# Three resumes fewer before the first convolution taps, block 0's transposes in the auxiliary banks, and a pair as first unit of the first paired feed-forward block

## The chip, the cores and the metric

The kernel runs on one core of a Trainium2 chip. The metric is the device time of one execution in microseconds. Before the change three runs gave a median of 1071.13 us (1070.79 to 1071.79). TensorE is called PE below, VectorE DVE, ScalarE ACT, GpSimd POOL, and the queue that issues nearly all DMAs SP.

## The reference

One layer of a hybrid encoder for a sequence of 256 rows of 2048 numbers, all in float32:

```python
xn = rms_norm(h, norm1_g[l])
proj = xn @ w_in                       # 5120 columns: q, k, v, ga, gg
att = diff_attention(rope(norm(q)), rope(norm(k)), v, lam)
u = ga * sigmoid(gg)                   # 1024 channels
u = causal_depthwise_conv(u, conv_w[l], conv_b[l])   # 31 taps
u = silu(layer_norm(u, conv_ln_g[l], conv_ln_b[l]))
h = h + concat([att, u]) @ w_out
hn = rms_norm(h, norm2_g[l])
h = h + (silu(hn @ w_gate) * (hn @ w_up)) @ w_down   # FFN_HIDDEN = 5632
```

## The kernel before, in words

**The matrix products.** The 256 rows are two row tiles m of 128. A weight is read from HBM once, in chunks of two k-tiles of 128 by 512 columns. Each chunk is split into a rounded part `hi` (ACT, L313) and the rest `lo = raw - hi` (DVE, L322); the activations are split in the same way. A product is then three matmuls, xhi by hi, xlo by hi (L352, L353) and xhi by lo (L358). A chunk has 12 matmuls of 512 columns on PE: eight in its first half, which need `hi` alone, and four in its second, which need `lo`.

**The order.** It is written out by the program itself: each engine runs its own list in the order in which the Python code emits it. `run_chunks` goes through a list of chunks; before the multiplication of chunk t it emits the load, the rounding and the splitting of chunks some places ahead (`lead`: 2 for plain chunks, 3 and 2 for the units of a paired block). What follows a block of products (gates, norms, transposes) stands in Python generators. `resume()` advances each running generator by one `yield`; it is called twice in a chunk, after the first and after the second half, so a `yield` is a delay of half a chunk in PE's list. `lag(n)` is n such delays. A chunk whose `prompt` is set gets one more `resume()` right behind its last one.

**Convolution.** The first four blocks of `w_in` give the gated channels, 256 at a time. `glu_done` takes a sigmoid (ACT), a product `u` (DVE, L475), transposes `u` on PE (`ps_u`, L483) and copies it to the padded buffer `upad` (ACT). From there on the 31 taps of each channel tile are queued in `side`, and DVE runs one tap (L495, 30 per channel tile, 240 in all) after the other between its other work, as a budget of DVE time per half chunk allows. When four channel tiles are through, `conv_back` transposes them back (`ps_y`, L516), and after the second four it takes the layer norm: statistics (DVE, L526 and L535), the reciprocal root (POOL, L210 to L540), scale and shift (ACT, L544), transposes (`ps_ln`, L553), SiLU (ACT, L557) and the split into `mchi` and `mclo` (DVE, L560, L561). The last chunks of `w_out` multiply `mchi` and `mclo`. The function `operand` emits what is missing of them right there, in front of the matmul that reads them.

**Feed-forward.** 5632 hidden columns are 11 blocks j of 512, in groups of 4, 4 and 3; after a group its rows of `w_down` are multiplied. Block 0 is plain: 8 chunks of `w_gate`, 8 of `w_up`, then `up_done` forms `a = up * rstd * silu(gate)` (DVE, L796), and `transposed` transposes it (`ps_a`, L809), rounds it (ACT, L811) and subtracts (DVE, L813). All other blocks are made by `fast_block` from 12 units: four `s` units (pairs), which multiply 4 k-tiles by 7 products of sums of operands (one level of a Strassen-like scheme over the two halves of k and the two weights), and four `g` and four `u` units, which are plain chunks of the other k-tiles. A pair has 21 matmuls on PE. It needs a 1 MB load (`wb`, two DMAs, L880), sums of the weights `wt` (DVE, L890 to L892), two roundings `wh` (ACT, L893 of `wb`, L896 of `wt`) and two subtractions `wl` (DVE, L898, L899). The operand side (`fhi`, `flo`, `chi`, `clo`) is made once, by `make_forms`, while block 0 runs. It reads the normed rows `hn`, whose two tiles lie in the two buffers that `wb` uses afterwards.

**PSUM.** Four banks `acc` and four banks `aux`. Plain blocks take two `acc` banks; a paired block takes the four `acc` banks for the products Q1, Q6, Q7, Q5 and the four `aux` banks for Q2, Q4, Q3, QX. Transposes use `aux`, but those of block 0 use `acc`.

```python
FIRST = "gugsgsusgsuu"      # units of block 1
ORDER = "sggsggsuusuu"      # units of blocks 2 to 10
PRODUCTS = ((Q1, 0, 5), (Q6, 5, 1), (Q7, 6, 2), (Q5, 4, 3), (Q2, 1, 6), (Q4, 3, 0), (Q3, 2, 4))
```

In `PRODUCTS` the third number is the row of `wh` and `wl` that is read: rows 4 to 6 come from L893 and L898, rows 0 to 3 from L896 and L899.

Of the kernel before, what the change touches and what calls it, by code (L numbers as in the profile page):

```python
# [12 lines left out]
F32 = mybir.dt.float32  # L13
# [5 lines left out]
P = 128  # L19
D = 2048  # L20
S = 256
# [49 lines left out]
FGROUPS = (4, 4, 3)  # L71
# [7 lines left out]

ORDER = "sggsggsuusuu"  # L80

FIRST = "gugsgsusgsuu"

Q1, Q6, Q7, Q5, Q2, Q4, Q3, QX = range(8)

PRODUCTS = ((Q1, 0, 5), (Q6, 5, 1), (Q7, 6, 2), (Q5, 4, 3), (Q2, 1, 6), (Q4, 3, 0), (Q3, 2, 4))

HI_AHEAD, LO_AHEAD = 3, 2

FIRSTS = [1] + [sum(FGROUPS[: g + 1]) for g in range(len(FGROUPS))]  # L90


def rope_constants():
# [10 lines left out]
def tile_block(  # L104
# [16 lines left out]
    acc_ps = ctx.enter_context(tc.tile_pool(name="acc", bufs=4, space=PSUM))  # L121
    aux_ps = ctx.enter_context(tc.tile_pool(name="aux", bufs=AUX, space=PSUM))
# [28 lines left out]
    def col(key, k):  # L151
        return cols[:, AT[key] + k : AT[key] + k + 1]
# [67 lines left out]
    def lhs_two(pfx, k):  # L220
        return tuple(lhs.tile([P, 2, S], F32R, tag=f"l{x}", name=f"{pfx}{x}{k}") for x in ("hi", "lo"))
# [21 lines left out]
    def lag(n):  # L243
        for _ in range(n):
            yield
# [4 lines left out]
    def room(n, hold=0):  # L250
        while held[0] + n > AUX:
            yield
        held[0] += hold
# [6 lines left out]
    def spend(us):  # L260
        credit[0] -= us
# [16 lines left out]
    chunks = []  # L278
# [182 lines left out]
    def glu_done(c0, nct, ps):  # L461

        w = nct * P
        while not normed:
            yield
        yield
        sig = []
        for m in range(NM):
            sig.append(pre.tile([P, HN], F32, tag="p1", name="sig"))
            act.activation(sig[m][:, :w], ps[m][:, :w], AF.Sigmoid, scale=rstd1[m])  # L470
        yield from lag(2)
        us = []
        for m in range(NM):
            u = pre.tile([P, HN], F32, tag="wt", name="u", bufs=4)
            dve.scalar_tensor_tensor(u[:, :w], ps[m][:, w:], rstd1[m], sig[m][:, :w], ALU.mult, ALU.mult)  # L475
            us.append(u)
        spend(0.25)
        yield from lag(3)
        yield from room(1)
        pt = aux_ps.tile([P, 2, S], F32, tag="aux", name="ps_u")  # L480
        for j in range(nct):
            for m in range(NM):
                pe.transpose(pt[:, j, m * P : (m + 1) * P], us[m][:, j * P : (j + 1) * P], ident)  # L483
        act.copy(upad[c0 // NB][:, c0 % NB : c0 % NB + nct, W - 1 :], pt[:, :nct])
        yield
        cts = range(c0, c0 + nct)
        for ct in cts:
            act.activation(y[:, ct, :], upad[ct // NB][:, ct % NB, :S], AF.Identity,  # L488
                           bias=col("cb", ct), scale=cw[:, ct, :1])
            side.append(deque((lambda k=k, ct=ct: tap(k, ct)) for k in range(1, W)))  # L490
# [298 lines left out]

    def up_done(j, ps):  # L790
        fp = ffn["pool"]
        yield
        aa = []
        for m in range(NM):
            a = fp.tile([P, N], F32, tag=f"sum{2 + m}", name="a")
            dve.scalar_tensor_tensor(a, ps[m], rstd2[m], sil[m], ALU.mult, ALU.mult)  # L796
            aa.append(a)
        yield
        yield from transposed(j, aa)

    def transposed(j, aa):
        last = j + 1 in FIRSTS
        for t in range(N // P // 2):
            pool_, tag = (aux_ps, "aux") if j else (acc_ps, "acc")
            pt = pool_.tile([P, 2, S], F32, tag=tag, name="ps_a")
            for i in range(2):
                for m in range(NM):
                    c = (2 * t + i) * P
                    pe.transpose(pt[:, i, m * P : (m + 1) * P], aa[m][:, c : c + P], ident)  # L809
            hi, lo = lhs_two("a", j * (N // P) + 2 * t)  # L810
            act.copy(hi, pt)  # L811
            yield from lag(1 if last else 2)
            dve.tensor_tensor(lo, pt, hi.bitcast(F32), ALU.subtract)  # L813
            for i in range(2):
                actT[j * (N // P) + 2 * t + i] = (hi[:, i, :], lo[:, i, :])
            yield from lag(1 if last else 4)
# [202 lines left out]
    c0 = 0  # L1019
    for nct in CONV_BLOCKS:  # L1020
        block(w_in, [(GC + c0 * P, nct * P), (AC + c0 * P, nct * P)], range(KD), fx,
              lambda ps, c0=c0, nct=nct: glu_done(c0, nct, ps))
# [13 lines left out]
    j0 = 0  # L1036
    for g, nb in enumerate(FGROUPS):
        for j in range(j0, j0 + nb):
            if j:
                fast_block(j, FIRST if j == 1 else ORDER, j == j0)  # L1040
                continue

            block(w_gate, j * N, range(KD), fh, silu_done)
            block(w_up, j * N, range(KD), fh, lambda ps, j=j: up_done(j, ps))
        for n in range(D // N):
            at = len(chunks)
            block(w_down, n * N, range(j0 * 4, (j0 + nb) * 4), fa, lambda ps, g=g, n=n: down_done(g, n, ps))
            for i, c in enumerate(chunks[at:]):
                c["prompt"] = True
                c["spare_raw"] = i % 3 == 2  # L1050
        j0 += nb
# [32 lines left out]
```

## Time and profile before

| what | value |
|---|---|
| median of 3 runs | 1071.13 us |
| the profiled execution | 1070.95 us, its span 1069.2 us, so 1.75 us lie around the span |
| busy, share of the span | ACT 55%, POOL 6%, DMA packets 62% of 16 engines' span |
| mean granted PE clock | 0.997 |
| convolution taps on DVE | 240 of 480 ns |

In rows of the timeline the first number is the start in us from the span's start, the second the duration, then engine, line, operation, output and inputs with their shapes and the count; in square brackets the idle time of that engine just before, and what ended it. Matmuls are pipelined: one of 512 columns shows about 0.39 us, and the next starts 0.227 us after it. A wait list has the engine and line that waited, what it waited for, and us in total, times, longest. A window table has, for each stretch, its length, the busy time of each engine with the number of instructions, the granted PE clock, the DMA share and GB/s.

### The profile page before, as it was taken

To read this page: it belongs to the slowest core of one execution; us is meant where nothing else is said; L and a number is where in the kernel's file an instruction comes from. 1 tells how busy PE (TensorE), PEld (TensorE's weight loads), DVE (VectorE), ACT (ScalarE), POOL (GpSimd) and SP (SyncE) were. 2 spreads that over 40 slices of the span, in tenths; PEclk is the share of its full clock that TensorE was granted. 3 is DMA by queue.
4 is the path that set the end of the run, shared out by engine and by line. 5 is a ranking of instruction groups with operands and counts; after the bars stand their busy time and mean duration, and the time that the engine had idled before them with its cause. 6 is when DMAs were issued, how large, how long until landed. Compare 5 with 4: busy or idle time off the path is not lost.

```text
span 1069.2 us, 13025 instructions
## 1 busy us (share of the span) xinstructions
PE 1052.4 (98%) x4738; PEld 865.6 (81%) x4738; DVE 842.8 (79%) x1022; ACT 588.8 (55%) x761; POOL 64.5 (6%) x101
## 2 busy tenths in 40 slices
PE   9999999999899998999999999999999999999998
PEld 7888888877688886778888888888888888888886
DVE  5699899898765589999664599999964579998653
ACT  6654566756656555466443465765643356646332
POOL 0030112201100000000000000000000000000000
PEclk9999999999999999999999999999999999999999
DMA  8756655544435556577555667867656568676661
GB/s 280 243 185 199 203 161 177 158 159 157 158 103 190 177 189 223 202 241 203 191 181 205 236 204 250 250 193 247 178 182 210 199 219 273 205 234 188 196 240 60
DMA packets 116812, 212.43 MB, mean 199 GB/s; under 512 B 7188, under 2 KB 25038, under 8 KB 116748
## 3 DMA queue, kind: packets, MB, share of 16 engines
q1 hardware_dynamic: 113616, 200.56, 55.7%
q0 software_dynamic: 3072, 11.01, 5.6%
q8 instruction: 37, 0.61, 0.2%
q14 instruction: 27, 0.22, 0.1%
q10 hardware_dynamic: 60, 0.03, 0.0%
HBM read 200.04 MB, written 2.10 MB: 189 GB/s over the span
## 4 chain that ended last, share of the span: by engine, by line
PE 84%; DVE 8%; ACT 3%; issue 2%; DMA 1%; POOL 1%; SPq 1%; DVEq 0%; ACTq 0%
PE acc L358 16%; PE acc L352 16%; PE acc L353 16%; PE q L932 6%; PE q L933 6%; PE q L938 6%; PE q L917 5%; PE q L915 5%; PE q L916 5%; DVE wlo L322 2%; DVE y L495 1%; PE ps_a L809 1%; ACT wh L896 1%; ACT whi L313 1%; DMA wb<-in_w_gate_dram 1%
## 5 line engine op out<-in xcount | busy, mean ns | idle before, releaser
L322 DVE TENSOR_TENSOR wlo<-raw,whi 128x1024 fp32r<-128x1024 f32 x278 | 337.6, 1222 | 141.7 <-ACT whi L313 141.6
L313 ACT CAST whi<-raw 128x1024 fp32r<-128x1024 f32 x296 | 309.1, 1052 | 235.3 <-PE acc L353 169.8
L352 PE MATMUL acc<-whi,ahi 128*128 128x512 f32 x384 | 150.0, 391 | 0.0
L353 PE MATMUL acc<-whi,alo 128*128 128x512 f32 x384 | 149.5, 389 | 0.0
L352 PE MATMUL acc<-whi,xhi 128*128 128x512 f32 x320 | 126.3, 395 | 0.6 <-ACT whi L313 0.4
L932 PE MATMUL q<-whi,chi 128*128 128x512 f32 x320 | 125.5, 392 | 0.0
L353 PE MATMUL acc<-whi,xlo 128*128 128x512 f32 x320 | 125.0, 391 | 0.3 <-DVE xlo L227 0.3
L933 PE MATMUL q<-whi,clo 128*128 128x512 f32 x320 | 124.7, 390 | 0.0
L896 ACT CAST wh<-wt 128x2048 fp32r<-128x2048 f32 x40 | 76.6, 1915 | 76.8 <-DVE wt L892 76.8
L915 PE MATMUL q<-wh,fhi 128*128 128x512 f32 x280 | 109.8, 392 | 0.7 <-DVE alo L813 0.7
L917 PE MATMUL q<-wl,fhi 128*128 128x512 f32 x280 | 109.2, 390 | 0.8 <-DVE wl L899 0.8
L916 PE MATMUL q<-wh,flo 128*128 128x512 f32 x280 | 109.0, 389 | 0.0
L495 DVE SCALAR_TENSOR_TENSOR y<-upad,cw,y 128x256 f32<-128x256 f32 x240 | 102.2, 480 | 2.6 <-ACT y L488 2.6
L358 PE MATMUL acc<-wlo,ahi 128*128 128x512 f32 x384 | 102.9, 389 | 0.0
L899 DVE TENSOR_TENSOR wl<-wt,wh 128x2048 fp32r<-128x2048 f32 x40 | 91.6, 2290 | 9.1 <-ACT wh L896 9.1
L358 PE MATMUL acc<-wlo,xhi 128*128 128x512 f32 x320 | 87.8, 396 | 0.9 <-DVE wlo L322 0.9
L938 PE MATMUL q<-wlo,chi 128*128 128x512 f32 x320 | 86.7, 393 | 0.0
L353 PEld LDWEIGHTS acc<-whi,alo 128*128 128x128 f32 x384 | 72.1, 188 | 14.9
L352 PEld LDWEIGHTS acc<-whi,ahi 128*128 128x128 f32 x384 | 72.1, 188 | 14.9
L358 PEld LDWEIGHTS acc<-wlo,ahi 128*128 128x128 f32 x384 | 72.0, 188 | 14.9
L352 PEld LDWEIGHTS acc<-whi,xhi 128*128 128x128 f32 x320 | 60.1, 188 | 13.7 <-ACT whi L313 0.8
L353 PEld LDWEIGHTS acc<-whi,xlo 128*128 128x128 f32 x320 | 60.1, 188 | 13.4 <-DVE xlo L227 1.1
(194 smaller groups left out, 1417.1 us busy)
## 6 DMA issues: line engine op xcount, KB each, us to landing
raw<-in_w_down_dram SPq DMA_DIRECT2D x88, 512.0 KB, 3.9
raw<-in_w_in_dram SPq DMA_DIRECT2D x48, 512.0 KB, 3.6
raw<-in_w_gate_dram SPq DMA_DIRECT2D x48, 512.0 KB, 4.6
raw<-in_w_up_dram SPq DMA_DIRECT2D x48, 512.0 KB, 3.6
wb<-in_w_up_dram SPq DMA_DIRECT2D x40, 512.0 KB, 3.8
wb<-in_w_gate_dram SPq DMA_DIRECT2D x40, 512.0 KB, 5.5
raw<-in_w_in_dram SPq DMA_DIRECT2D x64, 256.0 KB, 3.9
raw<-in_w_out_dram SPq DMA_DIRECT2D x32, 512.0 KB, 3.6
```

Source lines behind the costliest of these rows:

```text
L313: act.copy(c["hi"], c["raw"])
L322: dve.tensor_tensor(c["lo"], c["raw"], c["hi"].bitcast(F32), ALU.subtract)
L352: pe.matmul(ps[m], xhi[:, ms], hi[:, j, :], start=c["first"] and j == 0, stop=False)
L353: pe.matmul(ps[m], xlo[:, ms], hi[:, j, :], start=False, stop=False)
L358: pe.matmul(ps[m], xhi[:, ms], lo[:, j, :], start=False, stop=c["last"] and j == nk - 1)
L495: dve.scalar_tensor_tensor(y[:, ct, :], src, wk, y[:, ct, :], ALU.mult, ALU.add)
L915: pe.matmul(ps, fhi[:, f, p, :], c["hi"][:, w], start=bool(first), stop=False)
L916: pe.matmul(ps, flo[:, f, p, :], c["hi"][:, w], start=False, stop=False)
L917: pe.matmul(ps, fhi[:, f, p, :], c["lo"][:, w], start=False, stop=bool(last))
L932: pe.matmul(ps, x1[:, ms], hi[:, i, :], start=i == 0 and bool(c["first"].get(q)), stop=False)
L933: pe.matmul(ps, x2[:, ms], hi[:, i, :], start=False, stop=False)
L938: pe.matmul(sum_bank(c, q), forms["plain"][k][0][:, ms], lo[:, i, :], start=False, stop=i == 1 and bool(c["last"].get(q)))
```

## The change

Four edits:

1. For the first convolution block (c0 = 0) `glu_done` yields once instead of twice before `u` and once instead of three times before the transposes. Those stand 3 half chunks earlier in PE's list, directly behind the second half of the chunk that holds the transposes of the tap weights. All later work of the taps moves with it, as the queue of taps starts earlier.
2. `up_done` of block 0 has lost its `yield` at the start and its chunk is now `prompt`, so `a` is emitted right behind the last chunk; the transposes follow after `lag(4)` instead of one `yield`. They lie in `aux` banks.
3. `FIRSTS` no longer holds 1, so `transposed` of block 0 uses the longer delays (2 and 4) of the other blocks.
4. Block 1 has the unit order of all other blocks and begins with a pair instead of three plain units.

```diff
-FIRST = "gugsgsusgsuu"
-FIRSTS = [1] + [sum(FGROUPS[: g + 1]) for g in range(len(FGROUPS))]
+FIRSTS = [sum(FGROUPS[: g + 1]) for g in range(len(FGROUPS))]
...
             act.activation(sig[m][:, :w], ps[m][:, :w], AF.Sigmoid, scale=rstd1[m])
-        yield from lag(2)
+        yield from lag(2 if c0 else 1)
...
-        yield from lag(3)
+        yield from lag(3 if c0 else 1)
         yield from room(1)
         pt = aux_ps.tile([P, 2, S], F32, tag="aux", name="ps_u")
...
     def up_done(j, ps):
         fp = ffn["pool"]
-        yield
         aa = []
...
-        yield
+        yield from lag(4)
         yield from transposed(j, aa)
...
-            pool_, tag = (aux_ps, "aux") if j else (acc_ps, "acc")
-            pt = pool_.tile([P, 2, S], F32, tag=tag, name="ps_a")
+            pt = aux_ps.tile([P, 2, S], F32, tag="aux", name="ps_a")
...
-                fast_block(j, FIRST if j == 1 else ORDER, j == j0)
+                fast_block(j, ORDER, j == j0)
...
             block(w_up, j * N, range(KD), fh, lambda ps, j=j: up_done(j, ps))
+            chunks[-1]["prompt"] = True
```

How the lists move, at three places. The line numbers of the changed kernel are 2 to 4 lower.

DVE, end of the convolution, from the split of the last attention rows (`alo`) to the first operand of the convolution's product (`mchi`); before:

```order
L227 SCALAR_TENSOR_TENSOR alo_2771<-ps_at,cols,ahi_2770 128x256 x2
L495 SCALAR_TENSOR_TENSOR y<-upad_123,cw,y 128x256 x6
L322 TENSOR_TENSOR wlo<-raw,whi 128x1024
L495 SCALAR_TENSOR_TENSOR y<-upad_123,cw,y 128x256
L322 TENSOR_TENSOR wlo<-raw,whi 128x1024 x3
L526 BN_STATS stats_127<-upad_123 128x6
L526 BN_STATS stats_128<-upad_123 128x6
L322 TENSOR_TENSOR wlo<-raw,whi 128x1024
L535 BN_AGGR mv<-stats_127 128x2
L535 BN_AGGR mv<-stats_128 128x2
L322 TENSOR_TENSOR wlo<-raw,whi 128x1024 x2
L560 CAST mchi_2938<-z 128x256
```

and in the changed kernel:

```order
L225 SCALAR_TENSOR_TENSOR alo_2778<-ps_at,cols,ahi_2777 128x256 x2
L320 TENSOR_TENSOR wlo<-raw,whi 128x1024 x3
L524 BN_STATS stats_127<-upad_123 128x6
L524 BN_STATS stats_128<-upad_123 128x6
L533 BN_AGGR mv<-stats_127 128x2
L533 BN_AGGR mv<-stats_128 128x2
L320 TENSOR_TENSOR wlo<-raw,whi 128x1024 x2
L558 CAST mchi_2914<-z 128x256
```

The last seven taps (`y`) are gone from this place, as they ran earlier, and two chunk splits (`wlo`) fewer lie between `alo` and `mchi`.

PE, the last matmuls with attention rows (`alo`, `ahi`) and the first with the convolution's rows (`mchi`); before:

```order
L353 MATMUL acc<-whi,alo_2771 128x512
L358 MATMUL acc<-wlo,ahi_2770 128x512 x4
L553 MATMUL ps_ln<-ident,upad_122 128x128 x4
L352 MATMUL acc<-whi,mchi_2938 128x512
L353 MATMUL acc<-whi,mclo_2939 128x512
```

and in the changed kernel:

```order
L551 MATMUL ps_ln<-ident,upad_122 128x128 x4
L356 MATMUL acc<-wlo,ahi_2777 128x512 x4
L551 MATMUL ps_ln<-ident,upad_123 128x128 x4
L350 MATMUL acc<-whi,mchi_2914 128x512
L351 MATMUL acc<-whi,mclo_2915 128x512
```

The first fence's `ps_ln` is the first of four; in the second fence stand the second and the third, and the first stands a first half (eight matmuls) ahead of its top row. The transposes `ps_y` ahead of all this stand one and a half chunks earlier, so that five whole chunks lie between them and the first matmul with `mchi`, where there were three and the second half of one.

DVE, from the last of the operand forms (`flo`) to the second pair of block 1; before:

```order
L874 TENSOR_TENSOR flo<-sums,fhi 128x1536
L322 TENSOR_TENSOR wlo<-raw,whi 128x1024 x5
L890 TENSOR_TENSOR wt<-wb 128x1024
L891 TENSOR_TENSOR wt<-wb,wt 128x512
L892 TENSOR_TENSOR wt<-wt,wb 128x512
L322 TENSOR_TENSOR wlo<-raw,whi 128x1024
L796 SCALAR_TENSOR_TENSOR a<-acc,rstd_0_135,sil 128x512
L796 SCALAR_TENSOR_TENSOR a<-acc,rstd_1_136,sil 128x512
L898 TENSOR_TENSOR wl<-wb,wh 128x1536
L899 TENSOR_TENSOR wl<-wt,wh 128x2048
L813 TENSOR_TENSOR alo_3871<-ps_a,ahi_3870 128x512
L322 TENSOR_TENSOR wlo<-raw,whi 128x1024
```

and in the changed kernel:

```order
L870 TENSOR_TENSOR flo<-sums,fhi 128x1536
L320 TENSOR_TENSOR wlo<-raw,whi 128x1024 x3
L886 TENSOR_TENSOR wt<-wb 128x1024
L887 TENSOR_TENSOR wt<-wb,wt 128x512
L888 TENSOR_TENSOR wt<-wt,wb 128x512
L894 TENSOR_TENSOR wl<-wb,wh 128x1536
L895 TENSOR_TENSOR wl<-wt,wh 128x2048
L320 TENSOR_TENSOR wlo<-raw,whi 128x1024
L793 SCALAR_TENSOR_TENSOR a<-acc,rstd_0_135,sil 128x512
L793 SCALAR_TENSOR_TENSOR a<-acc,rstd_1_136,sil 128x512
L886 TENSOR_TENSOR wt<-wb 128x1024
L887 TENSOR_TENSOR wt<-wb,wt 128x512
```

The first pair's work (`wt`, `wl`) now directly follows the splits of the last three chunks of `w_up`, and `a` stands behind it and one more split.

## The prediction, made before the changed kernel had run

> **What bounds the kernel now.** I read the page's busy times first, then PE's list of waits, then the granted clock around the long waits, then the timeline there.
>
> ```profile
> span 1069.2 us, 13025 instructions
> ...
> PE 1052.4 (98%) x4738; PEld 865.6 (81%) x4738; DVE 842.8 (79%) x1022; ACT 588.8 (55%) x761; POOL 64.5 (6%) x101
> ```
>
> PE is busy for all but 16.8 us of the span and the change removes none of its matmuls, so only PE's stops can be won. PE's longest waits:
>
> ```profile
> PE acc L352 <- DVE mchi L560: 3.3, 1, 3.3
> PE ps_a L809 <- DVE a L796: 3.1, 2, 2.8
> ...
> PE q L917 <- DVE wl L899: 0.8, 1, 0.8
> PE q L915 <- DVE alo L813: 0.7, 1, 0.7
> ...
> PE ps_a L809 <- DVE sum L997: 0.3, 1, 0.3
> ```
>
> The first lies at the end of the convolution, the others around block 1; the change touches both places. Busy time hides a second cost, which the window table shows (the column after POOL is the granted clock):
>
> ```profile
> 287.10:290.50 3.40, 1.71 (x9) 1.00 (x7) 0.00 (x0) 3.40 (x5) 0.00 (x0) 1.00 0.47 172
> 290.50:293.90 3.40, 1.56 (x6) 1.11 (x7) 2.48 (x5) 1.24 (x3) 0.00 (x0) 1.00 0.00 1
> 293.90:297.30 3.40, 3.40 (x12) 2.71 (x11) 0.51 (x2) 1.02 (x2) 0.00 (x0) 0.50 0.00 0
> 403.10:406.50 3.40, 0.57 (x4) 0.15 (x2) 3.33 (x6) 2.16 (x3) 0.00 (x0) 1.00 0.78 295
> 406.50:409.90 3.40, 3.11 (x9) 2.40 (x10) 3.40 (x3) 2.83 (x3) 0.00 (x0) 0.51 0.03 8
> ```
>
> After each of the two long waits PE runs for 3.4 us at half its clock, which does 1.7 us less work. The window ahead of the slow one was busy for 1.56 and 0.57 us of 3.4; one with 1.71 us was not followed by a slow one. The two slow windows start 112.6 us apart, 33 times 3.41, so they lie on a fixed grid. I take half a window of idleness as the limit.
>
> **The change part by part.**
>
> *End of the convolution.* PE, then DVE:
>
> ```profile
> 278.00 1.04 PE L516 MATMUL ps_y<-ident,y 128*128 128x128 f32 x8
> ...
> 284.36 1.07 PE L358 MATMUL acc<-wlo,ahi 128*128 128x512 f32 x4
> ...
> 287.08 1.07 PE L358 MATMUL acc<-wlo,ahi 128*128 128x512 f32 x4
> ...
> 288.53 0.55 PE L553 MATMUL ps_ln<-ident,upad 128*128 128x128 f32 x3 [0.27 <-ACT upad L544]
> ...
> 292.34 0.49 PE L352 MATMUL acc<-whi,mchi 128*128 128x512 f32 x1 [3.26 <-DVE mchi L560]
> ```
>
> ```profile
> 269.40 1.27 DVE L495 SCALAR_TENSOR_TENSOR y<-upad,cw,y 128x256 f32<-128x256 f32 x3
> ...
> 273.14 2.46 DVE L495 SCALAR_TENSOR_TENSOR y<-upad,cw,y 128x256 f32<-128x256 f32 x6
> ...
> 276.65 0.48 DVE L495 SCALAR_TENSOR_TENSOR y<-upad,cw,y 128x256 f32<-128x256 f32 x1
> ...
> 292.00 0.28 DVE L560 CAST mchi<-z 128x256 fp32r<-128x256 f32 x1
> ```
>
> From `ps_y` (278.00) to the end of the first `mchi` (292.28) the chain of copy, statistics, root, shift, `ps_ln`, SiLU and cast takes 14.3 us. A chunk is 287.08 - 284.36 = 2.72 us of PE, so a matmul 0.227. In the new list `ps_y` stands 1.5 chunks earlier: 2.72 + 8 x 0.227 = 4.5 us, at 273.5. The taps allow it: the seven taken away here are those from 273.14 to 277.13, the last one left ends at 270.7. PE then has 0.8 (ps_y) + 5 x 2.72 + about 3 x 0.45 (three ps_ln) = 15.75 us of work before it needs `mchi`, 1.4 us more than the chain, in which two splits fewer now stand. So this stop goes. It cost 0.4 us of the interrupted `ps_ln`, then 292.34 less the 288.86 at which three transposes would have been through = 3.5, and 1.7 of clock: **5.6 us won**. Bounds: if the chain grew by 3 us, PE would stop for 1.6 and the clock might stay up, 4.0 won; the whole 5.6 is the most.
>
> *Opening.* The price of the earlier taps. PE, then DVE:
>
> ```profile
> 39.07 1.20 PE L358 MATMUL acc<-wlo,xhi 128*128 128x512 f32 x4
> ...
> 44.67 0.60 PE L483 MATMUL ps_u<-ident,u 128*128 128x128 f32 x4
> ```
>
> ```profile
> 39.28 0.87 DVE L475 SCALAR_TENSOR_TENSOR u<-acc,rstd,sig 128x256 f32<-128x256 f32 x2
> ...
> 47.05 1.67 DVE L495 SCALAR_TENSOR_TENSOR y<-upad,cw,y 128x256 f32<-128x256 f32 x4 [2.60 <-ACT y L488]
> ```
>
> `ps_u` now comes behind that L358, at 39.07 + 4 x 0.227 = 39.98, while the second `u` ends at 40.15: PE waits about 0.2, **0.2 lost** (bounds 0 and 0.5). ACT's copy of `ps_u`, which now waits there, holds up one rounding by less than a chunk, and roundings run two chunks ahead of PE. The first seven taps go into the 2.60 us in which DVE waited; as DVE's list between 47 and 270 is the same mixture, only seven taps ahead, I give it nothing.
>
> *Block 1: what goes.* PE:
>
> ```profile
> 398.89 0.39 PE L932 MATMUL q<-whi,chi 128*128 128x512 f32 x1
> ...
> 403.20 0.39 PE L933 MATMUL q<-whi,clo 128*128 128x512 f32 x1
> 406.41 0.36 PE L809 MATMUL ps_a<-ident,a 128*128 128x128 f32 x1 [2.83 <-DVE a L796]
> 407.07 0.90 PE L809 MATMUL ps_a<-ident,a 128*128 128x128 f32 x3 [0.29 <-DVE a L796]
> ...
> 415.86 0.50 PE L915 MATMUL q<-wh,fhi 128*128 128x512 f32 x1 [0.71 <-DVE alo L813]
> ...
> 460.16 0.50 PE L917 MATMUL q<-wl,fhi 128*128 128x512 f32 x1 [0.84 <-DVE wl L899]
> ```
>
> Idle counts from a modelled end, some 0.15 us after the next matmul could have started. Start to start, with 0.227 for a matmul and 0.1 for a transpose: 3.0 and 0.55 before `ps_a`, 1.7 of clock, 0.85 and 1.0 at the two last rows and 0.4 at the wait for L997: 7.5 us. In the new order `ps_a` stands behind a whole pair, when `a` is long done.
>
> *Block 1: what comes.* The pair now meets PE at 398.9, when `w_up` ends, instead of behind three plain units. DVE, ACT, and the landing times of `wb`:
>
> ```profile
> 384.61 1.28 DVE L869 TENSOR_TENSOR flo<-hn,fhi 128x512 fp32r<-128x512 f32 x2
> ...
> 391.12 4.62 DVE L322 TENSOR_TENSOR wlo<-raw,whi 128x1024 fp32r<-128x1024 f32 x4
> ...
> 401.88 1.23 DVE L890 TENSOR_TENSOR wt<-wb 128x1024 f32<-128x1024 f32 x1 [3.73 <-DMA wb<-in_w_gate_dram]
> ...
> 405.61 1.40 DVE L796 SCALAR_TENSOR_TENSOR a<-acc,rstd,sil 128x512 f32<-128x512 f32 x2
> 406.93 1.75 DVE L898 TENSOR_TENSOR wl<-wb,wh 128x1536 fp32r<-128x1536 f32 x1
> 408.60 2.28 DVE L899 TENSOR_TENSOR wl<-wt,wh 128x2048 fp32r<-128x2048 f32 x1
> ```
>
> ```profile
> 404.59 1.90 ACT L896 CAST wh<-wt 128x2048 fp32r<-128x2048 f32 x1 [1.24 <-DVE wt L892]
> ```
>
> ```profile
> DMA to landing us min/median/max: 3.4/4.5/9.9
> ```
>
> `wb` can start when L869 has read the first `hn` tile, at 385.3 to 385.9, and lands at some 391 (by the longest row 395.8). DVE has three splits first, 391.12 + 3 x 1.13 = 394.5, so the load is hidden. Then `wt`, 401.88 to the cast's start less 0.04, is 2.7 and ends at 397.2; `wl` L898 ends at 398.8, in time for the pair's first product. L896 takes 397.2 to 399.1, L899 thus 399.1 to 401.4. The second product's third matmul (row 1 of `wl`) is due at 398.89 + 5 x 0.227 = 400.0: **PE waits 1.4**. The third product needs an `acc` bank that `up` still holds until `a` has read it; behind L899 stand a split (1.13) and `a` (0.7): 403.15, while PE is there at 401.6: **PE waits 1.5**. The second `a` ends at 403.8, just when the fourth product comes. Queued behind on PE is only the pair itself; it ends near 406.7, and the following units' splits are ready by then.
>
> Is the clock lost here too? Idle is 2.9 us of 3.15, cut once by 0.23 us of matmul. With the limit of half a window, a grid of 3.4 us takes 1.8 us or more of it into one window in about 6 of 10 positions. So **1.7 us** more are lost.
>
> Sum: 5.6 + 7.5 - 0.2 - 2.9 - 1.7 = 8.3 us won. 1070.95 (profiled: span 1069.2 and 1.75 around it) - 8.3 = 1062.65; the median of the runs, 1071.13, is 0.2 higher, so 1062.7.
>
> Does DVE allow this? PE and DVE in the stage:
>
> ```profile
> 391.00:462.00 71.00, 65.98 (x285) 52.57 (x284) 64.32 (x61) 37.47 (x32) 1.03 (x1) 0.98 0.63 216
> ```
>
> DVE idles for 6.7 us of the 71, 3.73 of them in the wait for `wb` that goes. Without any idleness the `wl` at which PE waited until 460.16 would be there at 453.4. PE comes to it without the clock loss at 460.16 - 7.5 + 2.9 = 455.6, with it at 457.3. So no stop need remain there, but little more can be won in this stage.
>
> **The rivals.**
>
> *The clock stays up at the pair.* The stop falls on two windows, 1061.0. For it: the single long stops of 2.83 and 3.26 us are cut in two here. Against it: the 1.56 us of work in the window up to 293.90 were no protection. By the Trainium skill, "TensorE: Matmul & The Clock Gate", section "Part 1: The HAM clock gate (the "warmup" mystery)", the clock halves after an idle window of about 3.4 us; no such stop exists before or after, so by that rule the time would be 1061.0, yet the slow windows above followed stops shorter than that, and the trace decides.
>
> *The layer norm's chain stays late.* ACT's roundings of chunks in its list wait for PE, and POOL's four steps are uncertain; if 1.4 us of reserve are used up and 2.5 more, the time is 1065.2.
>
> *The first `wb` is late.* If it must wait until DVE has read both `hn` tiles (388.9) and takes the longest 9.9 us, it lands at 398.8; each us after 394.5 costs one: 4.3, 1067.0. Against it: SP has nothing else to issue there, since its next chunk waits for a buffer.
>
> *Slower than before.* The same load, held until the forms and the splits are through and then put behind other transfers: from a landing at 394.5 + 8.4 = 403 on, the wait at the pair eats all that is won; at 405 it would be 1073. For it: before the change DVE waited for this load until 401.88. Against it: it stood behind three more chunks in SP's list then.
>
> *Nothing measurable.* The chain's stop remains (5.6) and the pair's load is 2.5 us late: 1070.8.
>
> **How the numbers follow.** Forecast 0.40; clock stays up 0.30; chain late 0.11; load late by some us 0.10; nothing 0.05; slower 0.04. The range: 1060 at the bottom (the clock up and each wait 0.5 us shorter), at the top 1067, which takes in the late chain and the late load and leaves out the last two. A change of 0.2% (2.1 us) is about what a measurement of this kernel can tell from none: faster by more 0.91, within 0.05, slower 0.04.
>
> **What would show it.** No wait for `mchi` at L558 in the list of waits and clock 1.00 between 280 and 300 us. Near 393 to 398 (all is 5 us earlier) a wait of 1.4 us for `wl` L895 at the pair's second product and of 1.5 us for `a` L793 at the third, and after it at most one slow window. `ps_u` with a wait of 0.2 near 40. The forecast is wrong if the first `wt` waits for `wb`, if PE waits for `mchi` for over a us, or if a pair after the first stops PE.

## The result and the profile after

The changed kernel takes 1062.26 us (median of four runs, 1061.07 to 1062.69); the kernel before, beside it on the same chip, 1071.36 us (1070.79 to 1071.79). The ratio is 0.9914 with a 95% interval of 0.9896 to 0.9931: 9.1 us faster. A second set of five runs gave 1063.06 us and 0.9926 [0.9914, 0.9939]. The first median lies between two pairs of executions: 1061.07 and 1061.88 us with a mean granted clock of 1.000, 1062.64 and 1062.69 us with 0.998. The profiled execution of the changed kernel took 1061.07 us; it is one of those without a window of half clock, which matters below.

The page's head and busy times of the changed kernel:

```profile
span 1059.3 us, 13029 instructions
...
PE 1046.7 (99%) x4738; PEld 862.6 (81%) x4738; DVE 842.9 (80%) x1022; ACT 587.9 (56%) x761; POOL 65.2 (6%) x101
```

The span is 9.9 us shorter with the same 4738 matmuls. PE idles for 12.6 us instead of 16.8, so 4.2 us of the gain are stops. PE's busy time fell by 5.7 although its work is the same: before, matmuls ran through two windows at half clock, which cost 3.3 us (half of the 3.40 and 3.11 us of work in them). The remaining 2.4 cannot be put to a place, since the ends of matmuls are modelled and the border between busy and idle with them. PE's list of waits of the changed kernel:

```profile
...
PE q L913 <- DVE wl L895: 1.4, 1, 1.4
PE q L911 <- DVE a L793: 1.3, 1, 1.3
PE acc L350 <- ACT whi L311: 1.2, 1, 1.2
PE acc L356 <- DVE wlo L320: 0.9, 1, 0.9
```

The 3.3 for `mchi` and the 3.1 for `a` in front of `ps_a` are gone; the two upper rows are new. The two lower ones lie elsewhere: the third is at 6.92 us, in the opening, where the kernel before waits 0.4 and the second profiled execution of the changed kernel 0.4; the last, in the attention stage, is in the kernel before too.

**End of the convolution.** The timeline of PE, then of DVE, changed kernel:

```profile
273.70 1.03 PE L514 MATMUL ps_y<-ident,y 128*128 128x128 f32 x8
...
288.12 1.18 PE L356 MATMUL acc<-wlo,ahi 128*128 128x512 f32 x4
289.14 0.60 PE L551 MATMUL ps_ln<-ident,upad 128*128 128x128 f32 x4
289.50 0.48 PE L350 MATMUL acc<-whi,mchi 128*128 128x512 f32 x1
```

```profile
287.42 0.30 DVE L558 CAST mchi<-z 128x256 fp32r<-128x256 f32 x1 [0.65 <-ACT z L555]
...
288.09 0.29 DVE L558 CAST mchi<-z 128x256 fp32r<-128x256 f32 x1
```

PE comes to the first matmul with `mchi` at 289.50 without a stop; the cast was done at 287.72, 1.8 us ahead.

**Block 1's first pair.** PE, DVE and ACT of the changed kernel:

```profile
393.33 0.39 PE L911 MATMUL q<-wh,fhi 128*128 128x512 f32 x1
...
394.24 0.39 PE L912 MATMUL q<-wh,flo 128*128 128x512 f32 x1
395.98 0.50 PE L913 MATMUL q<-wl,fhi 128*128 128x512 f32 x1 [1.35 <-DVE wl L895]
397.78 0.50 PE L911 MATMUL q<-wh,fhi 128*128 128x512 f32 x1 [1.29 <-DVE a L793]
...
401.31 0.60 PE L805 MATMUL ps_a<-ident,a 128*128 128x128 f32 x4
```

```profile
388.98 1.22 DVE L886 TENSOR_TENSOR wt<-wb 128x1024 f32<-128x1024 f32 x1
...
393.63 2.29 DVE L895 TENSOR_TENSOR wl<-wt,wh 128x2048 fp32r<-128x2048 f32 x1 [0.31 <-ACT wh L892]
395.84 1.22 DVE L320 TENSOR_TENSOR wlo<-raw,whi 128x1024 fp32r<-128x1024 f32 x1
396.98 1.40 DVE L793 SCALAR_TENSOR_TENSOR a<-acc,rstd,sil 128x512 f32<-128x512 f32 x2
```

```profile
385.94 1.48 ACT L889 CAST wh<-wb 128x1536 fp32r<-128x1536 f32 x1 [0.82 <-DMA wb<-in_w_gate_dram]
```

`wb` landed at 385.9, 3.1 us before DVE turned to it at 388.98; DVE had no break, and PE stopped twice for DVE. `w_up` ends at 393.33, where it ended at 398.89 before: 5.56 us of the 9.9 are won by then, the rest in block 1. A second row marks the end of this part, the first matmul that was behind a wait for `wl` at 460.16 before:

```profile
450.22 0.50 PE L913 MATMUL q<-wl,fhi 128*128 128x512 f32 x1
```

It is 9.94 us earlier, and from there on nothing changes. So block 1 gave 9.94 - 5.56 = 4.4 us.

### The profile page after: what moved, and what is told of

It reads as the page before. It is cut to its first block, busy times and chain, and to the rows that moved or that the text cites. A ratio compares the mean times of both kernels' runs of the same rounds, so it can differ in the third digit from the quotient of the medians.

```text
span 1059.3 us, 13029 instructions
## 1 busy us (share of the span) xinstructions
PE 1046.7 (99%) x4738; PEld 862.6 (81%) x4738; DVE 842.9 (80%) x1022; ACT 587.9 (56%) x761; POOL 65.2 (6%) x101
## 4 chain that ended last, share of the span: by engine, by line
PE 88%; DVE 5%; ACT 3%; POOL 2%; issue 1%; DMA 1%; SPq 0%; DVEq 0%; ACTq 0%
PE acc L351 16%; PE acc L350 16%; PE acc L356 16%; PE q L928 7%; PE q L929 7%; PE q L934 7%; PE q L913 6%; PE q L911 6%; PE q L912 6%; DVE wlo L320 2%; DVE y L493 1%; PE ps_a L805 1%; ACT whi L311 1%; PE ps_o L705 1%; ACT junk L411 1%
## 5 line engine op out<-in xcount | busy, mean ns | idle before, releaser
L895 DVE TENSOR_TENSOR wl<-wt,wh 128x2048 fp32r<-128x2048 f32 x40 | 91.6, 2291 | 9.6 <-ACT wh L892 9.6
```

## The experiments

Each run is given against the kernel before on the same chip and in the same series. All times are medians with their lowest and highest.

| kernel | us | ratio to before, 95% interval |
|---|---|---|
| the changed kernel | 1062.26 (1061.07 to 1062.69) | 0.9914 [0.9896, 0.9931] |
| the changed kernel again | 1063.06 (1062.80 to 1064.15) | 0.9926 [0.9914, 0.9939] |
| only the convolution's edit | 1065.95 (1065.05 to 1066.68) | 0.9948 [0.9934, 0.9963] |
| only block 0's and block 1's edits | 1068.19 (1066.44 to 1070.76) | 0.9969 [0.9958, 0.9981] |
| delays 2 and 2 | 1064.06 (1063.16 to 1066.54) | 0.9934 [0.9917, 0.9950] |
| delays 2 and 1 | 1064.18 (1063.35 to 1065.03) | 0.9932 [0.9918, 0.9947] |
| a plain unit first | 1061.28 (1060.87 to 1064.10) | 0.9908 [0.9894, 0.9922] |
| other order of products | 1060.93 (1060.60 to 1061.14) | 0.9899 [0.9885, 0.9912] |
| two splits by DMA | 1062.71 (1061.90 to 1064.45) | 0.9919 [0.9905, 0.9933] |
| order of products and two splits by DMA | 1059.28 (1058.97 to 1059.81) | 0.9884 [0.9871, 0.9898] |
| the same, `a` ahead of a split | 1059.27 (1058.90 to 1059.66) | 0.9888 [0.9873, 0.9903] |
| plain unit first and two splits by DMA | 1060.53 (1060.23 to 1062.38) | 0.9904 [0.9891, 0.9918] |
| first `wb` late | 1071.81 (1069.77 to 1074.55) | 1.0002 [0.9991, 1.0012] |

My theory is that of the prediction: PE's stops and what they do to the clock are all that is won and lost. The rivals are a chain that does not get as short as worked out, and a DVE that is so full that each stop taken away returns elsewhere.

### The change in two halves

The kernel before with the convolution's delays alone:

```diff
-        yield from lag(2)
+        yield from lag(2 if c0 else 1)
...
-        yield from lag(3)
+        yield from lag(3 if c0 else 1)
```

> The kernel before with only the earlier taps of the first convolution block. Theory: the stop before mchi (3.3 us and a slow clock window) goes, ps_u costs 0.25 us, block 1 is as before with its slow window: 5.5 us faster than before, about 1065.9 us, one slow window (clock 0.998). Rival, the parts only work together: less than 4 us or more than 7 us.

1065.95 us, 5.6 us faster than before. PE's list of waits has no `mchi`; two waits of block 1 stand ahead of all others:

```profile
PE ps_a L809 <- DVE a L796: 2.7, 2, 2.3
PE q L915 <- DVE alo L813: 2.1, 1, 2.1
```

Block 1 was expected to be as before, with its slow window. In the profiled execution it has none: the window of the stop for `a` held 1.74 us of work, and the granted clock stays at 1.00. Still, from the end of `w_up` to the end of the span this execution takes only 0.5 us less than the kernel before (1063.3 - 393.53 = 669.8 and 1069.2 - 398.89 = 670.3), as the stop for `alo` has grown from 0.7 to 2.1 us. DVE's list shows why. From the landing of `wb` (`wt` starts at 401.88 before, at 396.02 here) to the `alo` that PE waits for (415.12 and 409.26) DVE works without a break, 13.24 us in both. So the load and DVE's list behind it set when PE gets past this row, and a slow window of PE ahead of it costs nothing by itself there.

The changed kernel with the old delays, that is everything but the convolution's edit:

```diff
-        yield from lag(2 if c0 else 1)
+        yield from lag(2)
...
-        yield from lag(3 if c0 else 1)
+        yield from lag(3)
```

> The changed kernel with the old delays of the first convolution block, so only the block 1 part is done. Theory: 4.5 us faster than before where the clock stays up at the first pair and 2.8 where it falls: 1066.9 or 1068.6 us; the stop before mchi with its slow window stays. Rival, the parts only work together: less than 2 us.

1068.19 us, 3.3 us faster. The stop for `mchi` is back as long as it was, beside the two new ones:

```profile
PE acc L350 <- DVE mchi L558: 3.3, 1, 3.3
...
PE q L913 <- DVE wl L895: 1.3, 1, 1.3
PE q L911 <- DVE a L793: 1.3, 1, 1.3
```

5.6 and 3.3 make 8.9; the whole change won 9.1 and, the second time, 8.3. The halves add up to within a us, so neither needs the other. Edits 2 to 4 were run only together; what each is worth alone is not shown.

### How long the layer norm's chain is

With delays between the old and the new ones, `u` stays where it was and the transposes come one, or two, half chunks earlier:

```diff
-        yield from lag(2 if c0 else 1)
+        yield from lag(2)
...
-        yield from lag(3 if c0 else 1)
+        yield from lag(3 if c0 else 2)
```

> The changed kernel, but the first convolution block's transposes only one half chunk earlier than before instead of three. Theory, the chain from ps_y to mchi has a fixed length and starts when the taps are through: it starts 1.8 us earlier, PE's stop before mchi is 3.3 - 1.8 = 1.5 us, and by the limit of half a window (1.7 us) the clock stays up there: 1.7 us slower than the changed kernel. Rival, the chain is held by something on its way (roundings that wait for PE, POOL): the stop stays near 3 us with its slow window, 5 us slower.

The first gives 1064.06 us, 1.8 over the changed kernel's first median where 1.7 was expected. PE's timeline has the stop at about half its length:

```profile
290.45 0.50 PE L350 MATMUL acc<-whi,mchi 128*128 128x512 f32 x1 [1.68 <-DVE mchi L558]
```

The window of that stop held 1.73 us of work, and the clock stays up behind it, as expected.

> The changed kernel, but those transposes two half chunks earlier than before instead of three. Theory: the chain starts 2.7 us earlier, PE's stop before mchi is about 0.4 us, so 0.4 us slower than the changed kernel, not to be told from it. Rival: a stop of 2 us or more remains.

(`lag(3 if c0 else 1)`, with `u` at `lag(2)`.) PE's timeline:

```profile
169.85 1.20 PE L356 MATMUL acc<-wlo,xhi 128*128 128x512 f32 x4 [0.78 <-DVE wlo L320]
...
220.48 1.21 PE L356 MATMUL acc<-wlo,xhi 128*128 128x512 f32 x4 [1.24 <-DVE wlo L320]
...
291.22 0.49 PE L350 MATMUL acc<-whi,mchi 128*128 128x512 f32 x1 [0.56 <-DVE mchi L558]
```

3.26, 1.68, 0.56 and none: each half chunk takes a piece off the stop, and the three half chunks of the change are the first number that removes it. That is the chain the prediction had timed. The time of the second run is a miss: I had expected 0.4 us more than the changed kernel, and its executions with an unbroken clock (1063.35 and 1063.49) lie about 2 us over the changed kernel's (1061.07 and 1061.88). The trace shows 1.2 us of it, beside the 0.56, in a profiled execution of 1065.03 us: splits that come late in the attention stage, 0.78 and 1.24 us where before and after have 0.85 once. The delay shifts which taps stand between which splits: directly in front of the first of these late splits stand four taps, where the changed kernel has three. That this is the whole cause of both stops is not shown. So moving the taps is not free of charge in the middle of the list; the prediction gave it nothing, and for the delays chosen that happened to hold.

### The two stops at block 1's first pair

In block 1 alone the first pair takes its products so that the three that need rows 4 to 6 (`wh` from L889, `wl` from L894) stand ahead, and the two whose `acc` banks wait for `a` at the end: Q1, Q2, Q3, Q6, Q4, Q7, Q5.

```diff
+        if j == 1:
+            units[0]["products"] = tuple(PRODUCTS[i] for i in (0, 4, 6, 1, 5, 2, 3))
```

> The changed kernel, but the first pair of block 1 multiplies first the three products that need neither the cast sums of the weights (rows 0 to 3 of wl) nor a bank held by w_up. In the changed kernel PE stops there for 1.35 and 1.29 us. Theory A, DVE is the bound of the stage: these stops shrink to about 0.1 and 0.9 us, but the wl of block 2's second pair, which came within 0.1 us of PE's need, is no earlier, so PE stops there for about 2 us; time within 0.5 us of the changed kernel where the clock stays up, and never a slow clock window. Rival B, the stops at the first pair are the whole loss: no new stop, 2.0 us faster than the changed kernel.

1060.93 us, and no execution of four with a slow window. The stop for `wl` at the pair is nearly gone, that for `a` half as long; at block 2's second pair PE now waits. PE's timeline:

```profile
398.24 0.50 PE L911 MATMUL q<-wh,fhi 128*128 128x512 f32 x1 [0.61 <-DVE a L793]
...
450.00 0.50 PE L913 MATMUL q<-wl,fhi 128*128 128x512 f32 x1 [0.82 <-DVE wl L895]
```

Of 2.6 us of stops 0.6 was left at their place, and 0.8 came back 52 us later; about 0.9 and 2 were expected. This agrees with the theory that DVE is the limit: in this stage it has hardly a break. The window table of the changed kernel, from block 1's start on:

```profile
385.30:456.30 71.00, 68.25 (x306) 55.29 (x305) 68.56 (x65) 39.51 (x34) 1.08 (x1) 1.00 0.65 212
```

DVE is busy for 68.56 of 71 us. So the next step takes work from it. In blocks 2 to 10 one plain chunk of each weight has its `lo` formed by a cast on ACT and an accumulating DMA instead of DVE's subtraction; here block 1 gets that too:

```diff
-                         ... by_dma=j > 1 and what in BY_DMA,
+                         ... by_dma=what in BY_DMA,
```

> As the kernel with the reordered products, and in addition block 1 lets the DMA queue of POOL form the lo part of two chunks, as the later blocks do, which takes 2 x 1.13 us from DVE. Theory A: the stop at block 2's second pair goes (DVE is there 2.3 us earlier), the stop at the first pair stays at about 1 us, so about 2 us faster than the changed kernel, near 1059.2 us with no slow clock window. Rival B: the DMA part adds nothing to the reordered products.

1059.28 us: faster than both kernels, its slowest execution (1059.81) ahead of all nine of the changed one. PE's list of waits:

```profile
...
PE acc L356 <- DVE wlo L320: 0.8, 1, 0.8
PE q L911 <- DVE a L793: 0.6, 1, 0.6
```

No wait for `wl` is left. The same splits by DMA without the order of products:

> The changed kernel with only the two chunks of block 1 moved from DVE to the DMA queue of POOL. Theory A: both stops at the first pair stay as they are, since the moved splits come after them; DVE reaches block 2's second pair 2.3 us ahead of PE, which wins nothing there: within 0.4 us of the changed kernel. Rival C, DVE's load as such sets the time of the stage: 2 us faster.

1062.71 us, no gain over the changed kernel: the two stops at the pair stay at 1.3 each, and whatever DVE has saved later finds no stop to remove. Against the first median of the changed kernel the two edits together are worth 3.0 us, the order alone 1.3 and the DMA alone nothing.

Part of that is the clock, as two of the four executions behind this median have a slow window. Profiled executions with the same clock can be compared from the end of `w_up` to the end of the span. Without a slow window the changed kernel takes 1059.3 - 393.33 = 666.0 us there, with the order 1059.2 - 393.80 = 665.4, and with both 1057.4 - 393.77 = 663.6. With one slow window the changed kernel takes 1061.3 - 393.84 = 667.5 and with the DMA alone 1060.9 - 393.75 = 667.2 (each is a single execution, so good to some tenths). So the order is worth 0.6, the DMA 0.3 and both 2.3 us; the rest of the 3.0 is the slow window that no longer comes.

A plain `g` unit in front of the pair gives DVE the time of 12 matmuls:

```diff
-                fast_block(j, ORDER, j == j0)
+                fast_block(j, "gsggsgsuusuu" if j == 1 else ORDER, j == j0)
```

> The changed kernel with one plain unit ahead of the first pair of block 1 (g s g g s g s u u s u u). Theory A: the plain unit's 2.72 us of PE cover the wait for wl and most of the wait for a (stops at the first pair under 0.5 us in all), and DVE being the bound of the stage gives 2 to 2.5 us of it back as stops at later pairs, so between 1 us faster and equal to the changed kernel, without a slow clock window. Rival B: 3 us faster.

1061.28 us. The stops at the pair go (0.17 left for `a`), and 0.85 for `wl`, 0.54 and 0.27 for `sum` come back behind. No slow window was expected, but one of the four executions took 1064.10 us at a mean clock of 0.998. With the splits by DMA added:

> The kernel that begins block 1 with one plain unit, and in addition two chunks of block 1 by DMA. Without the DMA part it had stops of 0.85, 0.54 and 0.27 us behind DVE at the end of block 1 and in block 2, and 0.17 at the first pair. Theory A, these three are DVE's load in the stage: they go, 1.5 us faster, about 1059.2 us; the 0.17 stays. Rival: they come from the order and stay, 1060.9 us.

1060.53 us where I had expected 1059.2. The stops for `wl` and `sum` are gone, but a new one has come. PE's timeline, then POOL's, then the row of the DMA issues in that stretch (KB each, median us from issue to landing):

```profile
416.55 1.20 PE L934 MATMUL q<-wlo,chi 128*128 128x512 f32 x4 [1.69 <-DMA wlo<-raw]
```

```profile
407.83 1.08 POOL L315 DMA_DIRECT2D wlo<-raw  x1 [46.02 <-ACT wlo L314]
```

```profile
wlo<-raw POOLq DMA_DIRECT2D x1, 512.0 KB, 8.7
```

The DMA that forms one of the two `lo` was issued at 407.83 and landed 8.7 us later; DVE's subtraction takes 1.22. In this order the unit comes up too soon for it.

Last, the stop for `a` that was left in the best kernel. `a` goes ahead of the split which DVE does before it:

```diff
-    lead = lambda t: (1, 1) if t < OPENING else (HI_AHEAD, LO_AHEAD) if "kind" in chunks[t] else (AHEAD, AHEAD)
+    lead = lambda t: (1, 1) if t < OPENING else (HI_AHEAD, LO_AHEAD) if "kind" in chunks[t] \
+        else (AHEAD, 1) if chunks[t]["w"] is w_up and chunks[t].get("prompt") else (AHEAD, AHEAD)
```

> The kernel with reordered products and two chunks by DMA in block 1, and DVE forms a ahead of the split of block 1's first plain chunk instead of behind it. Theory A, PE's last stop at the first pair (0.61 us) is the split's 1.13 us ahead of a: the stop goes, nothing else stops PE in block 1, 0.7 us faster than that kernel: about 1058.6 us, no slow clock window. Rival: the stop moves to the first plain chunk, whose split is now later: no gain.

1059.27 us, no gain. The stop for `a` has gone, and PE's timeline has another one at block 1's second pair:

```profile
407.06 0.50 PE L913 MATMUL q<-wl,fhi 128*128 128x512 f32 x1 [0.42 <-DVE wl L895]
```

The split and `a` have only changed places, so DVE is no earlier with what follows both: from the start of the first of the two to the second pair's `wt` it takes 2.45 us here (396.87 to 399.32) and 2.46 in the best kernel (396.29 to 398.75). In the best kernel the `wl` of this row was done at 406.42 and PE came to it at 406.77, 0.35 us later. A PE that no longer stops for 0.6 us at `a` is there too early.

### The price of a late load

The first `wb` of block 1 is loaded three times, one load behind the other, so that the last lands late:

```diff
+        for _ in range(3 if c["col"] == N and c["k"] == 0 else 1):
             for i, w in enumerate((w_up, w_gate)):
                 sp.dma_start(out=c["b"][:, 2 * i : 2 * i + 2, :], ...
```

> The changed kernel with the first load of block 1 (wb) issued three times, one behind the other, so that the copy which counts lands late; the result is the same. In the changed kernel the load lands at 385.9 and DVE needs it at 389.0. One load takes some 4 to 6 us from issue to landing, so the third should land at some 394 to 398, or 5 to 9 us after DVE is ready for it. Theory (the price that the prediction gave the rival 'the first wb is late': each us of lateness costs one us): DVE's wt waits for the DMA by 5 to 9 us, PE's stop at the first pair grows from 2.6 to 8 to 12 us, a window of half clock is certain, and the time is 5 to 9 us over the changed kernel's, 1068 to 1072, or no better than before. Rival (what follows the pair hides part of it, since DVE and SP gain room while PE stands): under half of the lateness is found in the time, 1064 to 1066. If the queue issues the three loads without waiting and they land together near 388, nothing changes, and the run says nothing on either.

1071.81 us, level with the kernel before. DVE's timeline, PE's timeline and the windows of this kernel:

```profile
397.22 1.22 DVE L887 TENSOR_TENSOR wt<-wb 128x1024 f32<-128x1024 f32 x1 [7.96 <-DMA wb<-in_w_gate_dram]
```

```profile
398.73 0.80 PE L912 MATMUL q<-wh,fhi 128*128 128x512 f32 x1 [5.04 <-ACT wh L890]
...
401.62 0.79 PE L914 MATMUL q<-wl,fhi 128*128 128x512 f32 x1 [1.67 <-DVE wl L895]
...
404.20 0.80 PE L914 MATMUL q<-wl,fhi 128*128 128x512 f32 x1 [0.94 <-DVE wl L896]
406.00 0.80 PE L912 MATMUL q<-wh,fhi 128*128 128x512 f32 x1 [1.00 <-DVE a L793]
```

```profile
394.94:398.36 3.42, 0.00 (x0) 0.00 (x0) 1.14 (x1) 1.16 (x1) 0.00 (x0) 0.99 1.05 404
398.36:401.77 3.41, 1.37 (x3) 0.66 (x3) 3.13 (x4) 2.16 (x3) 0.00 (x0) 0.50 1.05 390
401.77:405.18 3.41, 2.29 (x4) 1.01 (x4) 3.32 (x2) 3.32 (x4) 0.00 (x0) 0.50 1.05 379
405.18:408.60 3.42, 2.60 (x6) 2.12 (x7) 3.35 (x6) 0.00 (x0) 0.00 (x0) 0.50 0.87 272
408.60:412.01 3.41, 3.41 (x9) 2.65 (x9) 3.39 (x3) 0.00 (x0) 0.00 (x0) 0.51 0.18 21
```

DVE was held up by 8.0 us, and the span is 10.8 longer than that of the changed kernel's profiled execution, which has no slow window. Four windows ran at half clock, with 1.37 + 2.29 + 2.60 + 3.41 = 9.67 us of work in them, half of which is lost: 4.8. PE's stops came to 8.65 us instead of 2.64: 6.0 more. Together 10.8. So a late load is not forgiven later in the stage; the rival that DVE's and SP's room hides half of it has fallen. The time is 8.8 to 9.6 us over the two medians of the changed kernel, 1.1 to 1.2 us for each us of lateness; against an execution without a slow window it is 10.8 / 8.0 = 1.35.

### The clock at the pair

The changed kernel once more, to see how often its executions lose a window:

> The changed kernel once more, beside the two others. Theory: its executions fall in two groups by the granted clock, 1061.1 to 1061.9 us without a slow window (clock 1.0) and 1.7 us of work less, some 1062.6 to 1063.5, with one (0.998), in about 6 of 10; it is 3 to 4 us slower than the best of the kernels that do not stop at the pair.

1063.06 us; all five executions show a mean clock of 0.998 or 0.997, where one window at half clock takes 3.41 x 0.5 / 1061 = 0.0016 from it. So with the first four, 7 of 9 have a slow window and 2 have none. The slowest, 1064.15 us, lies outside the range that was expected. The window tables, on each execution's grid: first the profiled execution of the changed kernel (its grid is taken from the half clock that sets in behind its last matmul, at 1058.83), then the one of this second set.

```profile
393.24:396.66 3.42, 1.89 (x8) 1.00 (x6) 3.11 (x3) 3.42 (x4) 0.00 (x0) 1.00 1.04 387
396.66:400.07 3.41, 2.29 (x10) 1.89 (x11) 3.38 (x5) 0.21 (x1) 0.00 (x0) 1.00 0.86 278
```

```profile
396.14:399.55 3.41, 1.79 (x7) 1.22 (x8) 3.41 (x5) 1.20 (x1) 0.00 (x0) 1.00 0.89 293
399.55:402.97 3.42, 3.42 (x10) 2.65 (x9) 3.35 (x5) 0.00 (x0) 0.00 (x0) 0.50 0.32 122
```

It is the same list of instructions with the same two stops. Where the grid divides them as 1.89 and 2.29 us of work, the clock stays; where one window is left with 1.79, the next runs at half clock. The profiles of the other kernels fill the table in between:

| work of PE in a window that is otherwise at full clock, us of 3.41 | next window |
|---|---|
| 0, 0.55, 0.59, 0.83, 1.10, 1.49, 1.59 | half clock, each time |
| 1.71, 1.73, 1.74 | full clock, each time |
| 1.79 | half clock |
| 1.89, 1.91, 1.95, 2.09, 2.13, 2.29 | full clock, each time |

## Why the prediction was right, and where not

The forecast of 1062.7 (1071.13 less the 8.3 won is 1062.8) stands beside 1062.26 and 1063.06. That the first median comes so close is in part luck: with two executions in each group it lies between them, 0.4 from the nearest. The seven executions in which the forecast case came true have a median of 1063.01. By its steps:

**End of the convolution, 5.6 won.** The stop for `mchi` is gone and the clock is whole; measured are 5.6 us for this edit alone, with the opening's loss already off it, and in the trace 5.56 up to the end of `w_up` plus the 0.3 lost at the opening, 5.8. The chain took 14.0 us (273.70 to 287.72), predicted from the trace of before 14.3. PE had 15.8 us of work in that time, as worked out, and 1.8 in reserve instead of 1.4. The rival that the chain stays late needed 3.9 us more; nothing of that was seen.

**Opening, 0.2 lost.** PE's timeline of the changed kernel:

```profile
39.05 1.20 PE L356 MATMUL acc<-wlo,xhi 128*128 128x512 f32 x4
40.09 0.79 PE L481 MATMUL ps_u<-ident,u 128*128 128x128 f32 x4
40.64 0.48 PE L350 MATMUL acc<-whi,xhi 128*128 128x512 f32 x1
```

From 39.05 to 40.64 are 1.59 us; four matmuls take 0.91 and four transposes 0.4, so 0.28 are lost.

**Block 1, 7.5 won and 2.9 given back.** Start to start the two stops are 395.98 - 394.24 - 0.227 = 1.51 and 397.78 - 395.98 - 0.227 = 1.57, 3.1 instead of 1.4 + 1.5 = 2.9. In this execution without a slow window block 1 gave 4.4, the prediction's 7.5 - 2.9 = 4.6. Both stops came for the reasons named, `wl` of L895 and the `acc` bank that `a` frees. The order of the products showed it: with rows 4 to 6 ahead, the first stop went and the second shrank to 0.61. One step in the 7.5 is misread: it counts the slow window (1.7) and the stops up to `alo` as losses of their own, but the run with only the convolution's edit shows that the landing of `wb` and DVE's unbroken list behind it set the time of that row, with or without the window. As the change takes away both this late landing and the window, the total is right all the same. The run with only block 0's and block 1's edits gives the same gain in its profiled execution, whose clock stays up at the pair: 1065.2 - 399.29 = 665.9 us from the end of `w_up` on, 4.4 less than the 670.3 before.

**The clock, 1.7 lost in 6 of 10 positions.** 7 of 9 lost it, too few to tell 6 of 10 from 8 of 10. The share does not follow from the numbers beside it: of 2.9 us of idleness within 3.15 a window takes 1.8 or more in 7 of 10 positions; 6 of 10 comes out only with the shorter idle times that the profile shows (1.35 and 1.29 here). The price is a little smaller: the seven executions with a slow window have a median of 1063.01, the two without a mean of 1061.5, 1.5 apart. The likeliest case and the rival next to it (1061.0) were both there, in about the shares given, and their centres are 0.3 to 0.5 higher than predicted. The limit of half a window, on which the share rests, is only roughly right. A threshold in busy time alone would have to lie above 1.79 and below 1.71; the other readings all agree with half a window (1.706), that of 1.79 does not, and with modelled ends of matmuls it can't be said whether the limit or the reading is soft. The Trainium skill, "TensorE: Matmul & The Clock Gate", section "Part 1: The HAM clock gate (the "warmup" mystery)", gives a free-running window of 3413 ns, and the grid here agrees. Its condition, an idle window, does not: windows with 1.49, 1.59 and 1.79 us of work were followed by half clock.

**DVE: "no stop need remain there, but little more can be won in this stage".** The first half held, though with no room left. PE came to the row at 450.22 as DVE finished it; DVE's timeline of the changed kernel:

```profile
447.87 2.29 DVE L895 TENSOR_TENSOR wl<-wt,wh 128x2048 fp32r<-128x2048 f32 x1 [0.32 <-ACT wh L892]
```

It ends at 450.16. The prediction's earliest moment, 453.4 less the 5.5 won ahead of the stage, is 447.9; DVE still idled for 2.4 us in the stage (71.00 - 68.56), which is about the whole difference of 2.3. So the bound without idleness gave 2.2 us of room that did not exist. The second half was wrong: the best kernel wins 2.3 us more in the same stage at the same clock (3.0 by the medians), by sending two of DVE's subtractions elsewhere and by asking for its results later. I had read the room of DVE as fixed and had not asked what of its work other engines could do.

**The late load.** `wb` landed at 385.9, the prediction's 391 less 5.5 within half a us, and SP had nothing in its way. The price given to lateness, one us for each, was a little low: the medians give 1.1 to 1.2. In the trace it has two parts, 6.0 us of stops for 8.0 us of lateness, and 4.8 of clock, four slow windows instead of the one assumed. The break-even landing of the rival on the slower side, 8.4 us late, was nearly met by the 8.0 us of the experiment (ratio 1.0002 [0.9991, 1.0012]).

**What was expected of the experiments and missed.** In time three: the delays 2 and 1 (late splits in the attention stage), the plain unit first with the splits by DMA (the DMA takes 8.7 us), and `a` ahead of the split (the next pair's `wl` comes no earlier). Some met the time but not in every part: the convolution's edit alone (no slow window in block 1), the order of products (0.8 us at block 2's second pair, about 2 expected) and the plain unit first (an execution with a slow window). In the three misses the stop that I aimed at went or was as short as expected, and the same or another resource was late a little further on.

## What to carry to other kernels

Where PE is busy for 98% of the span, list its stops, and time each with the slow clock window that follows it; a removed stop of 3.3 us was worth 5.6. But where another engine's unbroken list sets the next stop, as in block 1 before the change, a slow window by itself costs nothing. When a stop is moved rather than removed, look which engine has to have its results ready there, and add up its busy time for the whole stage behind it: the bound without idleness was too kind here by about the idle time that DVE's own waits kept. A full engine gained here from two things together, results that are asked for in the order in which they come ready, and less work; at the same clock the one alone gave 0.6 us, the other 0.3, both 2.3.

## What was not expected of the hardware

The clock falls after windows that are far from idle, with up to 1.79 us of work in 3.41. Once it has fallen it does not come back after one window as long as PE has stops at half clock: after 1.37, 2.29 and 2.60 us of busy time at half clock a further slow window followed, after 3.41 not; in the kernel before (quoted with the prediction) one with 3.11 was enough, and with the two splits by DMA alone one with 3.08. The same program with the same stops thus falls into groups about 1.5 us apart, by where the grid lies.

The kernel before shows a mean clock of 0.997 in some executions and 0.995 in others, two or three slow windows; only an execution with two was looked at, so where the third lies stays open. Not settled either is the exact limit between 1.59 and 1.89 us of work.
